# A decoder trunk on one core: the second expert product runs on a gathered list of picked experts instead of on all expert blocks

## The chip, the cores and the metric

One core of a Trainium2 chip runs the whole program. The metric is the device time of one execution in microseconds (us). TensorE (PE) multiplies, VectorE (DVE) and ScalarE (ACT) do elementwise work, GpSimd (POOL) some more of it, and SyncE (SP) issues DMA transfers in the order of its program. All arrays are float32.

## What is computed

Two layers, each with three token mixers (a recurrent one and two kinds of attention) and then an expert layer, on 256 tokens of 1024 features. Only the expert layer is touched. In the reference it is this, run on two tiles of 128 tokens, with 8 heads, 128 x 128 = 16,384 experts and 16 picks for each head:

```python
def block(zb):                                   # 128 tokens
    q = (zb @ wq).reshape(128, 8, 2, 128)
    s = jnp.einsum('thpd,hpnd->thpn', q, subkeys)
    s_top, i_top = lax.top_k(s, 16)
    cand = (s_top[:, :, 0, :, None] + s_top[:, :, 1, None, :]).reshape(128, 8, 256)
    score, flat = lax.top_k(cand, 16)
    ...
    expert = i1 * 128 + i2
    gate = jax.nn.softmax(score, axis=-1)
    h = jnp.einsum('thkd,td->thk', u_tab[expert], zb)
    act = gate * jax.nn.gelu(h, approximate=False)
    return jnp.einsum('thk,thkd->td', act, v_tab[expert])
```

So a token uses at most 128 of the 16,384 rows of `u_tab` and `v_tab`. The kernel doesn't gather rows for each token: it makes a dense matrix of activations, experts by tokens, that is zero where a token didn't pick an expert, and multiplies it by all of `v_tab`.

## The kernel before

Every float32 product is made of three products of rounded parts (`mm3`, L284 to L286): a value is split into a rounded `hi` (ScalarE, a cast) and the rest `lo` (VectorE, a subtraction), both at L280, and TensorE adds hi by hi, hi by lo and lo by hi. Weights come from memory in pieces of 128 x 1024 values, 512 KB: SP issues the load at L244 into a ring of `raw` tiles (3 slots), `load_split` splits it into `hi` and `lo` (2 sets, and a further set called `third` in part of the V phase), and a `raw` slot is free for the next load when its `lo` is made.

The expert layer (`peer`, L1044) has these stages, one after the other on TensorE:

- The query weights `wq` and the routing (`route`): scores, the top picks of each token, their gates. It leaves `sl` (which picks) and `gp` (the gates).
- The U phase, one `expert_h` (L1104) for each block of 128 experts, 128 blocks: a `ut` piece is loaded and split, 24 matmuls of 128 x 256 follow, and Gelu goes to the activations `HA` (blocks 0 to 47) or `HB` (48 to 127), experts on partitions, 256 tokens each.
- Beside the U phase, from block `SPLIT` = 48 on, `gate_map` (L1218): for each quad of tokens, VectorE makes one-hot rows (`oh`, L1233) and multiplies by the gates (L1236), TensorE makes 8 small f16 matmuls (L1241), which give the gate of each expert and token, and the activations are multiplied by it (L1244, L1248, L1250). There are 64 quads. `Pace` lets out 1.8 units of this work for each U block, and a quad costs 1.8, so one quad stands beside one block until they are used up. The later blocks are plain.
- The V phase, `accum` (L1000): for each of the 128 blocks, a `v` piece is loaded and split, the activations are split into `ah` and `al` (`a_of`, 2 buffers each), and 12 matmuls of 128 x 512 add to four accumulators, one for each token tile and half of the 1024 features (`sc`, `sc`, `tp`, `po`). Expert blocks are 128 rows of `v` in their order.

The order of instructions on each engine is set when the program is built, by a list scheduler that runs a timeline of its own, except where the code orders some explicitly. SP's DMAs take turns on 8 completion semaphores.

Of the kernel before, what the change touches and what calls it, by code (L numbers as in the profile page):

```python
# [21 lines left out]
L = 2  # L22
# [19 lines left out]
LAG = 1  # L42
ORDER = "rsrrrsrrcsrcrrrnrccrcsrcrrscrncsrrrgnrrrnaagSaSaSSagSgSaggSnggggSagSSnSaagaaaSgSgmSSSamamaSSaagSggSgggggSSmgmmgmmmmmmmmmmmmmmmmmm"
# [64 lines left out]

def layout(a):
# [36 lines left out]
    for h in range(H):  # L146
# [5 lines left out]
    c, hot, ext, iota = constants()  # L152
    d = dict(
# [4 lines left out]
        ut=a["peer_u"].reshape(L, NB, P, 8, P).transpose(0, 1, 4, 3, 2),  # L158
        v=a["peer_v"].reshape(L, NB, P, D),
# [9 lines left out]
        cst=c, eye=np.eye(P, dtype=np.float32), hot=hot, ext=ext, iota=iota,  # L169
# [26 lines left out]
class Kernel:  # L196
# [39 lines left out]
    def load(self, src):  # L236
        raw = self.ring.tile([P, D], F32, tag="raw", name="raw", bufs=RAW)
        n = 1
        for s in src.shape[1:]:
            n *= s  # L240
        v = raw[:, :n]
        if len(src.shape) == 3:
            v = v.rearrange("p (a b) -> p a b", a=src.shape[1])
        self.nc.sync.dma_start(v, src)  # L244
        return v

# [797 lines left out]
    def peer(self, l):  # L1044
        nc, I = self.nc, self.I
        act, dve, pe = nc.scalar, nc.vector, nc.tensor
        with ExitStack() as ctx:
# [26 lines left out]
            self.hdone, self.tok = 0, 0  # L1074
            run = Pace(self.gate_map(hp, (sl, gp), HA, HB), PACE_G)
            for b in range(SPLIT, NB):
                self.expert_h(l, b, blk(b), hp, self.tok)
                self.hdone += 1
                run(1)
            run(None)  # L1080

            def a_of(b):
                ah = hp.tile([P, T], F32R, tag="ah", name="ah", bufs=2)
                al = hp.tile([P, T], F32R, tag="al", name="al", bufs=2)
                self.split(blk(b), ah, al)
                return ah, al
# [4 lines left out]
            if l + 1 == self.layers:  # L1091
# [4 lines left out]
            self.xnew = self.accum(lambda b: I["v"][l, b], NB, a_of, lambda: self.load_x(self.xd[0]),  # L1096
                                     l + 1 < self.layers)
# [3 lines left out]
            if l + 1 == self.layers:  # L1101
                self.final(self.xnew, lnf)

# [9 lines left out]
    def route(self, rp, sub, qT, slots):  # L1113
# [21 lines left out]
        for t in range(2):  # L1135
# [29 lines left out]
            for n in range(2):  # L1165
# [12 lines left out]
                if n == 0:  # L1178
# [11 lines left out]
                    yield 0.8  # L1190
            gt = rp.tile([P, H, 16], F32, name="gt")
# [26 lines left out]
    def gate_map(self, hp, slots, HA, HB):  # L1218
# [7 lines left out]
        nc.gpsimd.tensor_copy(iota2, iota[:, :, None].to_broadcast([P, P, 2]))  # L1226
        for t0 in range(0, T, 4):
# [8 lines left out]
            dve.tensor_tensor(og, oh[:, 0:1].to_broadcast([P, 2, 2, P, 2]),  # L1236
                              g[:, :, :, None].to_broadcast([P, 2, 2, P, 2]), op=OP.mult)
            p = self.pt([P, 4, P], "sc")
            for j in range(4):
                for n in range(2):  # L1240
                    pe.matmul(p[:, j], lhsT=oh[:, 1, j // 2, :, j % 2], rhs=og[:, n, j // 2, :, j % 2], start=n == 0,  # L1241
                              stop=n == 1)
            pv = p.rearrange("p t i -> p i t")
# [8 lines left out]
            yield 1.8  # L1252

# [27 lines left out]
```

## Time and profile before

| what | before |
|---|---|
| median of 3 runs (lowest, highest) | 2372.96 us (2371.32, 2373.24) |
| the profiled execution: its time | 2373.9 us |
| its span, first to last instruction | 2372.1 us |
| TensorE busy | 2339.2 us, 99% of the span |
| VectorE, ScalarE, GpSimd busy | 72%, 50%, 3% |
| layer 0: `gate_map` matmuls, first to last quad | 540 to 792 us |
| layer 0: V matmuls | 836.80 to 1185.59 us |
| layer 1: V matmuls | 2013.41 to 2364.65 us |

Of the views, the table by stretch of time gives for each engine how long it was busy, the granted TensorE clock (1.00 is full speed), the share of time in which the 16 DMA engines were busy, and the rate at which data moved. The tables of instruction groups give a line, an engine, an operation, the tiles written and read, a count, the total and the mean time. TensorE's records overlap, because matmuls are pipelined, so the price of one matmul is read from the distance between starts.

### The profile page before, as it was taken

What the parts mean: (1) busy time and instruction counts of PE and PEld (TensorE: products, weight loads), DVE (VectorE), ACT (ScalarE), POOL (GpSimd) and SP (SyncE); (2) the same over time, 40 slices, a digit from 0 to 9 for tenths busy, and PEclk for the clock granted to TensorE, in tenths of its full rate; (3) what the DMA queues carried; (4) which work ended last, traced back from release to release, by engine and by line L of the source; (5) the groups of instructions that cost most, each with busy time, mean ns of one, the idle gap of its engine ahead of it and who ended that gap; (6) DMA issues with size and microseconds to landing.
All of it is one profiled execution on the core that took longest, in us unless ns stands there. A gap on an engine that the chain in (4) does not pass through costs nothing.

```text
span 2372.1 us, 43631 instructions
## 1 busy us (share of the span) xinstructions
PE 2339.2 (99%) x16838; PEld 2111.2 (89%) x16838; DVE 1698.7 (72%) x3691; ACT 1181.1 (50%) x2269; POOL 73.2 (3%) x107
## 2 busy tenths in 40 slices
PE   8999999999999999999999999999999999999998
PEld 8888889999999988888888888899999999888887
DVE  6678577995899666666666785779958996566665
ACT  5544344554444455555555443345545444555554
POOL 0001030000000000000000010300000000000000
PEclk9999899999999999999999998999999999999999
DMA  5643246555455566666645432455555555666664
GB/s 187 201 147 104 68 125 197 163 183 177 155 152 160 169 213 195 192 192 194 194 164 183 141 106 64 148 184 161 179 178 154 159 154 184 209 192 194 195 195 152
DMA packets 126008, 395.23 MB, mean 167 GB/s; under 512 B 25270, under 2 KB 30824, under 8 KB 125544
## 3 DMA queue, kind: packets, MB, share of 16 engines
q1 hardware_dynamic: 125512, 391.92, 53.1%
q8 instruction: 132, 2.16, 0.4%
q14 instruction: 76, 0.62, 0.1%
q10 hardware_dynamic: 288, 0.52, 0.1%
HBM read 387.39 MB, written 5.01 MB: 165 GB/s over the span
## 4 chain that ended last, share of the span: by engine, by line
PE 91%; DVE 4%; DMA 2%; ACT 1%; issue 1%; POOL 0%; SPq 0%; DVEq 0%; POOLq 0%; ACTq 0%
PE mm L284 16%; PE mm L286 15%; PE mm L285 15%; PE sc L285 6%; PE sc L286 5%; PE sc L284 5%; PE sc L1241 3%; PE tp L286 3%; PE tp L285 3%; PE po L285 3%; PE po L286 3%; PE tp L284 3%; PE po L284 3%; DVE lo L280 2%; PE sc L837 1%; DMA raw<-wa 1%
## 5 line engine op out<-in xcount | busy, mean ns | idle before, releaser
L280 ACT CAST hi<-raw 128x1024 fp32r<-128x1024 f32 (+1 forms) x609 | 637.4, 1048 | 679.5 <-PE mm L285 494.0
L280 DVE TENSOR_TENSOR lo<-raw,hi 128x1024 fp32r<-128x1024 f32 (+1 forms) x609 | 748.3, 1230 | 303.2 <-ACT hi L280 301.4
L284 PE MATMUL mm<-zh,hi 128*128 128x256 f32 x3056 | 885.9, 290 | 6.2 <-ACT HA L1107 3.7
L286 PE MATMUL mm<-zh,lo 128*128 128x256 f32 x3056 | 875.1, 286 | 3.3 <-DVE lo L280 3.3
L285 PE MATMUL mm<-zl,hi 128*128 128x256 f32 x3056 | 868.6, 284 | 0.0
L284 PEld LDWEIGHTS mm<-zh,hi 128*128 128x128 f32 x3056 | 587.6, 192 | 25.3 <-issue 11.8
L286 PEld LDWEIGHTS mm<-zh,lo 128*128 128x128 f32 x3056 | 586.7, 192 | 13.5 <-issue 5.7
L285 PEld LDWEIGHTS mm<-zl,hi 128*128 128x128 f32 x3056 | 587.7, 192 | 3.8 <-issue 2.9
L280 DVE TENSOR_TENSOR third<-raw,third 128x1024 fp32r<-128x1024 f32 x80 | 98.0, 1225 | 50.6 <-ACT third L280 50.6
L280 ACT CAST ah<-HB 128x256 fp32r<-128x256 f32 x160 | 65.2, 407 | 121.5 <-PE po L285 121.5
L280 DVE TENSOR_TENSOR al<-HB,ah 128x256 fp32r<-128x256 f32 x160 | 68.0, 425 | 76.5 <-PE po L286 76.5
L285 PE MATMUL sc<-lo,ah 128*128 128x512 f32 x362 | 115.8, 389 | 0.1
L284 PE MATMUL sc<-hi,ah 128*128 128x512 f32 x362 | 115.4, 389 | 0.0
L286 PE MATMUL sc<-hi,al 128*128 128x512 f32 x362 | 112.4, 389 | 0.0
L280 ACT CAST third<-raw 128x1024 fp32r<-128x1024 f32 x80 | 84.3, 1054 | 44.8 <-PE po L286 36.4
L1233 DVE TENSOR_TENSOR oh<-iota,sl 128x1024 f16<-128x1024 f16 x128 | 87.5, 685 | 6.2 <-PE sc L1241 4.2
L1236 DVE TENSOR_TENSOR oh<-oh,gp 128x1024 f16<-128x1024 f16 x128 | 87.3, 683 | 0.0
L1241 PE MATMUL sc<-oh 128*128 128x128 f16 x1024 | 81.5, 220 | 0.0
L285 PEld LDWEIGHTS sc<-lo,ah 128*128 128x128 f32 x362 | 67.9, 188 | 14.6 <-DVE lo L280 0.6
L286 PEld LDWEIGHTS sc<-hi,al 128*128 128x128 f32 x362 | 67.9, 188 | 14.0
L284 PEld LDWEIGHTS sc<-hi,ah 128*128 128x128 f32 x362 | 67.8, 188 | 14.0
L280 ACT CAST ah<-HA 128x256 fp32r<-128x256 f32 x96 | 38.8, 406 | 65.7 <-PE po L285 65.7
(420 smaller groups left out, 3617.3 us busy)
## 6 DMA issues: line engine op xcount, KB each, us to landing
raw<-ut SPq DMA_DIRECT2D x256, 512.0 KB, 3.6
raw<-v SPq DMA_DIRECT2D x256, 512.0 KB, 3.5
raw<-wa SPq DMA_DIRECT2D x102, 512.0 KB, 3.3
raw<-wq SPq DMA_DIRECT2D x32, 512.0 KB, 3.6
raw<-wbr SPq DMA_DIRECT2D x24, 512.0 KB, 3.5
raw<-cw SPq DMA_DIRECT2D x16, 512.0 KB, 4.1
raw<-wo SPq DMA_DIRECT2D x16, 512.0 KB, 4.7
btile<-bd SPq DMA_DIRECT2D x16, 256.0 KB, 4.3
```

Of the source, the lines that this page charges most:

```text
L280: return self.nc.scalar.copy(hi, src), self.nc.vector.tensor_tensor(lo, src, hi.bitcast(F32), op=OP.subtract)
L284: return [mm(p, lhsT=l[0], rhs=r[0], start=first, stop=False), mm(p, lhsT=l[0], rhs=r[1], start=False, stop=False), mm(p, lhsT=l[1], rhs=r ...
L285: mm(p, lhsT=l[0], rhs=r[1], start=False, stop=False),
L286: mm(p, lhsT=l[1], rhs=r[0], start=False, stop=last)]
L837: pe.matmul(p, lhsT=qs(j), rhs=keys[lo:lo + 64, 0:nbr, 0:n], start=True, stop=True)
L1233: dve.tensor_tensor(oh.rearrange("p n a i j -> p (n a) i j"), iota2[:, None].to_broadcast(full), two(sl), op=OP.is_equal)
L1236: dve.tensor_tensor(og, oh[:, 0:1].to_broadcast([P, 2, 2, P, 2]), g[:, :, :, None].to_broadcast([P, 2, 2, P, 2]), op=OP.mult)
L1241: pe.matmul(p[:, j], lhsT=oh[:, 1, j // 2, :, j % 2], rhs=og[:, n, j // 2, :, j % 2], start=n == 0, stop=n == 1)
```

## The change

The V phase multiplies, for each token tile, only rows that some token of that tile picked.

- The rows of `ut` and `v` are turned on the host: row r of block b goes to place (r + b) mod 128 of its block, so that one column of picks spreads over the partitions. `route` computes the same turned place (three more VectorE instructions).
- `gate_map` has 4 more matmuls for each quad (L1385). They add to `cnt`, which says for each expert and token tile whether somebody picked it.
- `lists` (L1399) follows the quads. On the 116 first blocks it classes each expert as picked by both tiles, by one only, or by none, ranks the experts of each class inside groups of four partitions, and sorts them: 15 `max` and 14 `match_replace` of 128 x 464 values, some 25 small VectorE instructions, and a few small matmuls. `rows` and `vrows` come out: for each partition a list of 116 row numbers, those of tile 0 only first, then both, then tile 1 only. `flag` is over zero when the classes don't fit the fixed lengths below.
- `keep` writes the finished activations of blocks 0 to 115 to `act` in memory, by SP, in pieces of 8 blocks by 128 tokens (512 KB, rows of 512 bytes). The first half of the tokens is written once 128 tokens are gated, the second after all 256.
- `experts_out` takes the place of `accum` here. 12 dense blocks (116 to 127) run first, with 12 matmuls each as before. Then 106 gathered items: item j takes column j of `rows`. GpSimd issues two indirect DMAs for each: 128 rows of `v` (4 KB each) and 128 rows of `act` (1 KB each), into slots laid out in `HA`'s room, 7 for `v` and 10 for `act`. Items 20 to 79 serve both token tiles (12 matmuls), items 0 to 19 tile 0 only and 80 to 105 tile 1 only (6 matmuls each), mixed evenly. Columns 106 to 115 are left out.
- Ahead of the 43rd item every engine reads `flag` and branches: the branch's body does what the fixed lengths leave out (396 matmuls, with single buffers), and is skipped when `flag` is zero.

The V phase has then 12 x 12 + 60 x 12 + 46 x 6 = 1140 matmuls of 128 x 512 in place of 1536.

```diff
+ND = 12
+NC = NB - ND
+FROM1, TO0, TO1 = 20, 80, 106
+IF_AT = 42
+CHUNK = 8
...
+    def gather(self, src, row, dst):
+        self.nc.gpsimd.indirect_dma_start(out=dst, out_offset=None, in_=src,
+                                          in_offset=bass.IndirectOffsetOnAxis(ap=row, axis=0))
...
+            def keep():
+                for h in range(2):
+                    if self.tok < P * (h + 1):
+                        continue
+                    ready = min(SPLIT + self.hdone, NC)
+                    while kept[h] < ready:
+                        b = kept[h]
+                        n = min(CHUNK, (SPLIT if b < SPLIT else NC) - b)
+                        if b + n > ready:
+                            break
+                        src = HA[:, b:b + n] if b < SPLIT else HB[:, b - SPLIT:b - SPLIT + n]
+                        nc.sync.dma_start(dA[b * P:(b + n) * P, h * P:(h + 1) * P].rearrange("(b p) t -> p b t", p=P),
+                                          src[:, :, h * P:(h + 1) * P])
+                        kept[h] += n
...
                 self.expert_h(l, b, blk(b), hp, self.tok)
                 self.hdone += 1
                 run(1)
+                keep()
             run(None)
...
-            self.xnew = self.accum(lambda b: I["v"][l, b], NB, a_of, lambda: self.load_x(self.xd[0]),
-                                     l + 1 < self.layers)
+            self.xnew = self.experts_out(l, hp, HA, blk, dA, l + 1 < self.layers)
...
+                raw, src = (cut(7 + n % 2, D), cut(46 + n % 2, T)) if rest else (cut(n % 7, D), cut(36 + n % 10, T))
+                self.gather(I["v"], self.vrows.bitcast(U32)[:, b:b + 1], raw)
+                self.gather(dA, self.rows.bitcast(U32)[:, b:b + 1], src)
+                if rest or n % 3 == 2:
+                    w = third[:, 0], third[:, 1]
+                else:
+                    w = [self.ring.tile([P, D], F32R, tag=tag, name=tag) for tag in ("hi", "lo")]
+                self.split(raw, *w)
...
+        for b in range(NC, NB):
+            both(ready(b, (0, 1), True))
+        self.deep = False
+        ahead = []
+        for n, (b, ts) in enumerate(seq):
+            if n == IF_AT:
+                ahead = [ready(*seq[n + k]) for k in range(2)]
+                flag = nc.values_load(self.flag, min_val=0, max_val=1 << 20)
+                with self.tc.If(flag > 0):
+                    for j in range(FROM1):
+                        both(ready(j, (1,), rest=True))
+                    for j in range(TO0, TO1):
+                        both(ready(j, (0,), rest=True))
+                    for j in range(TO1, NC):
+                        both(ready(j, (0, 1), rest=True))
+            both(ahead.pop(0) if ahead else ready(b, ts))
...
-            dve.tensor_tensor(og, oh[:, 0:1].to_broadcast([P, 2, 2, P, 2]),
-                              g[:, :, :, None].to_broadcast([P, 2, 2, P, 2]), op=OP.mult)
+            for n in range(2):
+                dve.tensor_tensor(og[:, n], oh[:, 0], g[:, n, :, None].to_broadcast([P, 2, P, 2]), op=OP.mult)
...
+                at = t0 + j
+                pe.matmul(cnt[:, at // P], lhsT=oh[:, 1, j // 2, :, j % 2], rhs=oh[:, 0, j // 2, :, j % 2],
+                          start=at % P == 0, stop=at % P == P - 1)
...
+        yield from self.lists(hp, cnt)
```

SP's order before, layer 0, from the end of the routing to the end of the V loads (tiles are named target first; `ut`, `v`, `wa` are weights, and x90 is 90 issues in a row):

```order
L244 DMA raw<-ut 128x1024 x38
L1225 DMA iota<-iota 128x128
L244 DMA raw<-ut 128x1024 x90
L244 DMA raw<-wa 128x1024
L244 DMA raw<-v 128x1024 x21
L232 DMA xt<-xd_116 128x1024 x2
L244 DMA raw<-v 128x1024 x107
```

and after, from the loads ahead of token 256 to the dense `v` loads (ahead of these rows, after the load that follows token 128, 6 writes from `HA` and 4 from `HB` stand in one row, and three more between the loads):

```order
L267 DMA raw<-ut 128x1024 x7
L1116 DMA act_6692<-HA 128x8x128 x5
L1116 DMA act_6692<-HB 128x8x128
L1116 DMA act_6692<-HA 128x8x128
L1116 DMA act_6692<-HB 128x8x128 x8
L267 DMA raw<-ut 128x1024 x3
L1116 DMA act_6692<-HB 128x4x128 x2
L1209 TENSOR_LOAD flagi
L1209 ISA x2
L267 DMA raw<-ut 128x1024 x8
L267 DMA raw<-wa 128x1024
L267 DMA raw<-v 128x1024 x12
```

The 90 loads in a row are cut up: 10 writes stand in a row ahead of the load that follows token 128, 15 in a row ahead of the load that follows token 256, and a read of the flag stands ahead of the last 8 `ut` loads.

VectorE at the second of those places, before (the last quads of layer 0, with a block's `lo` and its activation product `HB<-HB,gel` beside each):

```order
L1236 TENSOR_TENSOR oh<-oh,gp 128x1024
L1244 SCALAR_TENSOR_TENSOR HA<-HA,sc 128x48x4
L1248 SCALAR_TENSOR_TENSOR HB<-HB,sc 128x63x4
L280 TENSOR_TENSOR lo<-raw,hi 128x1024
L1111 TENSOR_TENSOR HB<-HB,gel 128x252
L1244 SCALAR_TENSOR_TENSOR HA<-HA,sc 128x48x4
L1248 SCALAR_TENSOR_TENSOR HB<-HB,sc 128x64x4
L280 TENSOR_TENSOR lo<-raw,hi 128x1024
```

and after (`ms`, `cf`, `off`, `over` belong to `lists`), from the last `lo` that stands ahead of the 15 writes' load:

```order
L307 TENSOR_TENSOR lo<-raw,hi 128x1024
L1247 TENSOR_TENSOR HB<-HB,gel 128x256 x2
L1432 TENSOR_TENSOR ms<-ms,off 128x464
L1449 TENSOR_SCALAR over<-off 128x1
L1450 TENSOR_SCALAR over<-off 128x1
L1451 TENSOR_SCALAR over<-off 128x1
L1433 TENSOR_TENSOR ms<-ms 128x464
L1435 TENSOR_REDUCE cf<-ms 128x116
L1438 TENSOR_SCALAR ms<-cf 128x116
L1439 TENSOR_SCALAR ms<-ms 128x116
L1440 TENSOR_SCALAR ms<-ms 128x116
L1247 TENSOR_TENSOR HB<-HB,gel 128x256
```

Here 32 instructions of the lists and of `HB` stand between two `lo`, and a part of the sort has come ahead of the next one.

GpSimd, which issued no DMA before, has this order behind the routing (layer 0; the pairs of the last two rows go on to the end of the phase):

```order
L1366 CAST iota_6725<-iota 128x256
L271 DMA HA<-act_6692,rows 128x256 x5
L271 DMA HA<-v,vrows 128x1024 x6
L271 DMA HA<-act_6692,rows 128x256
L271 DMA HA<-v,vrows 128x1024
L271 DMA HA<-act_6692,rows 128x256 x4
L271 DMA HA<-v,vrows 128x1024
L271 DMA HA<-act_6692,rows 128x256
L271 DMA HA<-v,vrows 128x1024
```

All of the V phase's loads but 12 have moved from SP's queue to GpSimd's.
## Rows read from the trace of the kernel before

**Rows 1.** Page, part 1: busy us (share of the span) and instructions of each engine.

```profile
PE 2339.2 (99%) x16838; PEld 2111.2 (89%) x16838; DVE 1698.7 (72%) x3691; ACT 1181.1 (50%) x2269; POOL 73.2 (3%) x107
```

**Rows 2.** Stretches of layer 0: U with quads, plain U, V (columns in the first line).

```profile
core 0: us, PE busy (x) PEld busy (x) DVE busy (x) ACT busy (x) POOL busy (x), PEclk, DMA share, GB/s
540.00:780.00 240.00, 240.00 (x2222) 237.42 (x2221) 197.88 (x371) 114.77 (x266) 0.00 (x0) 1.00 0.54 161
800.00:836.00 36.00, 34.86 (x291) 34.66 (x290) 18.14 (x25) 15.99 (x24) 0.00 (x0) 1.00 0.55 181
1000.00:1170.00 170.00, 170.00 (x751) 140.77 (x750) 103.02 (x126) 91.47 (x126) 0.00 (x0) 1.00 0.63 193
```

**Rows 3.** Waits of SP's queue: for whom, us in total, times, longest us.

```profile
SPq L244 <- DVE lo L280: 975.5, 361, 16.9
```

**Rows 4.** Timeline of PE, layer 0: start us, us, instruction; a quad, then V's ends.

```profile
779.93 0.28 PE L286 MATMUL mm<-zh,lo 128*128 128x256 f32 x1
...
781.01 0.28 PE L286 MATMUL mm<-zh,lo 128*128 128x256 f32 x1
781.14 0.63 PE L1241 MATMUL sc<-oh 128*128 128x128 f16 x8
781.58 0.36 PE L284 MATMUL mm<-zh,hi 128*128 128x256 f32 x1
...
836.80 0.63 PE L284 MATMUL sc<-hi,ah 128*128 128x512 f32 x2
...
1185.20 0.39 PE L286 MATMUL po<-hi,al 128*128 128x512 f32 x1
```

**Rows 5.** Waits of PE: for whom, us in total, times, longest us.

```profile
PE mm L325 <- DVE diag L323: 9.2, 4, 7.2
```

**Rows 6.** DMA issues: count, KB each, median us to landing.

```profile
raw<-ut SPq DMA_DIRECT2D x256, 512.0 KB, 3.6
raw<-v SPq DMA_DIRECT2D x256, 512.0 KB, 3.5
...
xd<-xt SPq DMA_DIRECT2D x6, 512.0 KB, 2.6
```

**Rows 7.** Page, part 5: instructions xcount | busy us, mean ns of one | idle before.

```profile
L280 ACT CAST hi<-raw 128x1024 fp32r<-128x1024 f32 (+1 forms) x609 | 637.4, 1048 | 679.5 <-PE mm L285 494.0
L280 DVE TENSOR_TENSOR lo<-raw,hi 128x1024 fp32r<-128x1024 f32 (+1 forms) x609 | 748.3, 1230 | 303.2 <-ACT hi L280 301.4
...
L280 DVE TENSOR_TENSOR al<-HB,ah 128x256 fp32r<-128x256 f32 x160 | 68.0, 425 | 76.5 <-PE po L286 76.5
```

**Rows 8.** A further instruction group of DVE, the same columns.

```profile
L1214 DVE MATCH_REPLACE8 S<-top,S 128x128 f32<-128x128 f32 x64 | 17.0, 277 | 0.0
```

**Rows 9.** Another stretch, the same columns as rows 2: loads in the mixer of layer 1.

```profile
1256.00:1259.40 3.40, 3.40 (x24) 2.63 (x23) 1.36 (x4) 1.85 (x4) 0.00 (x0) 1.00 0.86 325
```

**Rows 10.** Instruction groups of POOL, the same columns as rows 7.

```profile
L979 POOL TENSOR_TENSOR mg<-mg,gate 128x256 f32<-128x256 f32 x32 | 32.9, 1034 | 58.9 <-DVE st L699 32.0 <-DVE gate L977 26.9
...
L314 POOL TENSOR_TENSOR ss<-ss,neghalf 128x1 f32<-128x1 f32 x10 | 5.5, 554 | 1348.1 <-DVE ss L313 1346.4 <-DVE small L379 1.7
```

**Rows 11.** Tile blk: duration ns min/median/max of one line on DVE and on POOL.

```profile
L542 DVE TENSOR_TENSOR TQ<-blk,cst x4: 1225/2096/2973, 196.7 to 1378.4; 128x1024 f32<-128x1024 f32 x4
L542 POOL TENSOR_TENSOR TQ<-blk,cst x4: 2915/2919/2922, 196.8 to 1380.3; 128x1024 f32<-128x1024 f32 x4
```

**Rows 12.** Timeline of PE at the start of the span.

```profile
7.16 1.23 PE L325 MATMUL mm<-diag,xt 128*128 128x128 f32 x4 [7.16 <-DVE diag L323]
8.18 1.06 PE L325 MATMUL sm<-diag,xt 128*128 128x128 f32 x4
9.03 1.06 PE L325 MATMUL mm<-diag,xt 128*128 128x128 f32 x4
...
11.92 0.61 PE L325 MATMUL mm<-diag,xt 128*128 128x128 f32 x4
12.37 0.61 PE L325 MATMUL sm<-diag,xt 128*128 128x128 f32 x4
```

More of the change, by code (lines that the diff above doesn't have):

```diff
@@ L106, in constants, with quads @@
     return c, hot, ext, np.tile(i.astype(f), (P, 1))
+def quads():
+    i = np.arange(P)
+    same = i[:, None] % 32 == i[None, :] % 32
+    m = i // 32
+    q = np.zeros((P, 7, P), np.float32)
+    q[:, 0] = same & (m[:, None] < m[None, :])
+    q[:, 1] = same & (m[:, None] > m[None, :])
+    for n in range(4):
+        q[:, 2 + n] = same & (m[:, None] == n)
+    q[:, 6, :NC] = NC * 512 + m[:, None] * P + np.arange(NC)
+    q[:, 6, NC] = -65536.0 * m
+    q[:, 6, NC + 1] = 1.0
+    return q
 def layout(a):
@@ L152, in layout @@
     c, hot, ext, iota = constants()
+    turn = (r(P)[None, :] - r(NB)[:, None]) % P
+    skew = lambda w: w.reshape(L, NB, P, D)[:, r(NB)[:, None], turn]
     d = dict(
@@ L157, in layout @@
         wq=cols(a["peer_wq"], r(2048)),
-        ut=a["peer_u"].reshape(L, NB, P, 8, P).transpose(0, 1, 4, 3, 2),
-        v=a["peer_v"].reshape(L, NB, P, D),
+        ut=skew(a["peer_u"]).reshape(L, NB, P, 8, P).transpose(0, 1, 4, 3, 2),
+        v=skew(a["peer_v"]).reshape(L * NB * P, D),
         subk=a["peer_subkeys"].reshape(L, 16, P, P).transpose(0, 3, 1, 2),
@@ L168, in layout @@
         rel=a["rel_bias"],
-        cst=c, eye=np.eye(P, dtype=np.float32), hot=hot, ext=ext, iota=iota,
+        cst=c, eye=np.eye(P, dtype=np.float32), hot=hot, ext=ext, iota=iota, quad=quads(),
+        low=np.tile((r(P) % 32).astype(np.int32)[:, None], (1, NC)),
     )
@@ L1073, in peer @@
             blk = lambda b: HA[:, b] if b < SPLIT else HB[:, b - SPLIT]
-            self.hdone, self.tok = 0, 0
+            dA = self.dram.tile([NC * P, T], F32, name=f"act{l}")
+            self.l, self.hdone, self.tok = l, 0, 0
+            kept = [0, 0]
+            def keep():
[12 more added lines that the diff above has]
+                        kept[h] += n
             run = Pace(self.gate_map(hp, (sl, gp), HA, HB), PACE_G)
@@ L1079, in peer @@
                 run(1)
+                keep()
             run(None)
[L1082 to L1086, printed above, removed]
+            keep()
+            assert kept == [NC, NC]
             if l + 1 < self.layers:
@@ L1190, in route @@
                     yield 0.8
+            dve.tensor_tensor(e, e, i1, op=OP.add)
+            wrap = rp.tile([P, H, 16], F32, name="wrap")
+            dve.tensor_scalar(wrap, e, float(P), float(P), op0=OP.is_ge, op1=OP.mult)
+            dve.tensor_tensor(e, e, wrap, op=OP.subtract)
             gt = rp.tile([P, H, 16], F32, name="gt")
@@ L1226, in gate_map @@
         nc.gpsimd.tensor_copy(iota2, iota[:, :, None].to_broadcast([P, P, 2]))
+        cnt = self.pt([P, 2, P], "tp")
         for t0 in range(0, T, 4):
```

142 lines of the change are left out of this document (added).

## The prediction, made before the changed kernel ran

> **What bounds the kernel now.** I read the page's busy times first: TensorE multiplies for 99% of the span, and no other engine is busy over 72% [rows 1]. So time goes only where matmuls go, unless something new makes TensorE wait. Then the three stretches of layer 0 [rows 2]: TensorE is busy 240 of 240 us beside the quads and 170 of 170 us in V, at the full granted clock; VectorE has 18% free beside the quads, half in the plain U blocks, 39% in V; the DMA engines are busy 0.54 to 0.63 of the time. SP mostly waits for a ring slot [rows 3], so loads come when room is there, and memory isn't what limits. What I must ask is which of these reserves the change eats up.
>
> The sum is made against the profiled execution, 2373.9 us (span 2372.1); the median of the runs is 0.9 us lower. All terms are for one layer, and there are two.
>
> **Matmuls taken away.** V runs from 836.80 to 1185.59 us, 348.8 us for 1536 matmuls, 0.227 us each [rows 4]. 396 fewer: **-89.9 us**. This holds if TensorE still goes at its own pace: 1140 matmuls then take 259 us, the mean gathered item 996 x 0.227 / 106 = 2.13 us.
>
> **Matmuls added.** A quad's 8 small matmuls begin at 781.14 and the next block's at 781.58: 0.055 us each [rows 4]. 256 more: **+14.1 us**, on TensorE in a stretch where it has no gap [rows 2]. The split gate product costs VectorE no more elements, and the routing's three extra instructions lie where I see no wait of TensorE's over 7.2 us in all of the span [rows 5]: 0.
>
> **The writes of the activations.** A queue is served in SP's order: 10 writes stand ahead of a `ut` load at token 128, 15 at token 256. Their price isn't in the trace. At the V loads' share, 0.63 busy at 193 GB/s [rows 2], full engines would move 306 GB/s (193/0.63), and 512 KB takes 1.71 us. TensorE's cover is the three `raw` slots: a block is 24 x 0.12 = 2.88 us, with its quad now 3.5 us [rows 4]. Token 128: 10 x 1.71 - 3 x 3.5 = 7 us. Token 256: 15 x 1.71 - 3 x 2.88 = 17 us. Together **+24 us**. Bounds: with two more blocks of cover in `hi` and `lo`, 0 and 11 us; with writes in 512-byte rows at half the pace, 24 and 43 us. I stay at 24, because the one large write seen lands no later than a load, 2.6 against 3.6 us [rows 6]. The other five writes stand alone among loads: 0.
>
> **The lists.** They are VectorE work behind the last quad, and TensorE doesn't need them before the gathers. An instruction of 256 values takes 0.425 us, one of 1024 1.230 us, and a match_replace of 128 0.277 us [rows 7, 8], so one of 464 about 0.64 us (an estimate from these). 36 of these and some 18 small ones at 0.27: 28 us. The 16 plain blocks last 46 us and leave VectorE half free, 23 us [rows 2]; the second stall adds 17. So the lists hide behind a stall that is paid already: **0**. Without that stall they would cost 28 - 23 = 5 us themselves. SP's read of the flag waits for them too, but the loads behind it need slots that VectorE frees later still.
>
> **The gathers.** 12 dense blocks (12 x 2.72 = 33 us) run while the first 17 gathers are issued. Then an item needs 640 KB and two gathers. VectorE needs 1.23 + 0.43 = 1.66 us of 2.13 [rows 7]. DMA at 306 GB/s needs 2.14 us, just TensorE's pace; where the engines were busiest they moved 325 GB/s at 0.86 [rows 9], that is 378 GB/s and 1.73 us. If the 1 KB rows of `act` cost double for each byte, the item takes 2.57 us at the lower rate: 0.44 x 106 = +47 us; at the higher rate nothing is lost. I take **+10 us**, near the cheap end, because the busiest row is the one most like a queue that is never empty. GpSimd's own price for a gather isn't in the trace either. Its instruction on one value for each partition takes 0.554 us, on 256 values 1.034 us, on 1024 values 2.919 us [rows 10, 11]. A gather reads one value for each partition, so the nearest rows are the first two: at 1.034 us GpSimd would finish V in 30 + 195 x 1.034 + 8 = 240 us (30 until the slots come free in turn, 195 gathers still to issue, 8 for the end), less than 259: it hides.
>
> By the Trainium skill's "DMA: Bandwidth & Descriptors", section "Latency and other measured facts", such a DMA has a first byte after about 1 us, put down there to the descriptors being made in software; by that price V is 30 + 195 + 8 = 233 us and the sum the same. No run so far shows it.
>
> **The branch.** All engines empty their queues around it and GpSimd waits until its gathers have landed. TensorE has two items in hand, 4.3 us. Bounds: the 1.1 us that it lost where U turns into V (36.00 - 34.86) [rows 2], and a load plus a split, 3.5 + 1.0 + 1.2 = 6 us [rows 6, 7]. I take **+4 us**.
>
> **Slow starts.** After its one long wait TensorE ran four matmuls in 1.02 and 0.85 us, and from about 11 us on in 0.45 us [rows 12]: 3.7 us at half its pace, 1.8 us lost. Three stalls a layer: **+5 us** (0 to 7).
>
> **Sum.** -89.9 + 14.1 + 24 + 0 + 10 + 4 + 5 = -32.8 us a layer, -66 us in both: 2308 us.
>
> **Rival 1: GpSimd makes descriptors slower than that.** V is then 38 + 195p for a price p of one gather. It decides from 259 us on, p = 1.13; the whole gain is gone when V takes 259 + 10 + 32.8 = 302 us, p = 1.35. At p = 1.6: 350 us, 91 - 10 = 81 us more, +48 a layer, **2470 us**, slower. For it: 1.35 lies between two rows, and 212 gathers of 128 rows each are much for an engine that is busy 3% now. Against it: a gather doesn't read 256 values. Chance 0.15.
>
> **Rival 2: VectorE and GpSimd shut each other out.** The same subtraction took VectorE 1.225 us or up to 2.973 us when GpSimd ran its half beside it, 2.919 us [rows 11]: one waited for the other. In V both work all the time: VectorE's `lo` and `al` and GpSimd's two gathers. One after the other an item takes 1.66 + 2 x 0.554 = 2.76 us, V 33 + 106 x 2.76 = 326 us, 67 - 10 = 57 us more: +24 a layer, **2422 us**, slower. It decides when the part of a gather that holds VectorE off is over 0.44 us ((302 - 33) / 106 = 2.54; (2.54 - 1.66) / 2). [...] Chance 0.11.
>
> The Trainium skill's "SBUF — State Buffer", section "Who interferes with whom", says that a VectorE instruction with two inputs in SBUF, such as these subtractions, contends with a GpSimd one that reads SBUF, and that the second to start blocks fully. That speaks against this change; rows 11 agree with it for elementwise work, and none shows it for a gather. By this rule the whole gather counts, and the time is the 2422 us above.
>
> **Rival 3: the writes are absorbed.** SP's writes overlap loads, the two stalls cost 0 and 5 us (the lists), one slow start is left: -89.9 + 14.1 + 5 + 10 + 4 + 2 = -55 a layer, **2264 us**. For it: the DMA engines are busy 0.55 of the time in U [rows 2], and the order leaves loads in flight. Chance 0.23.
>
> **Rival 4: it doesn't do what it says, because the branch is taken.** 396 matmuls come back, as 56 items with one buffer each: load, split and multiply in turn, at least 1.0 + 1.2 + 1.4 us each, 3.6 x 56 = 202 us more: some 2710 us. Worked out from the reference on its inputs, the classes fit in both layers with some per cent to spare (at least 92 rows for tile 0 only of every four partitions, 80 needed; at most 411 picked at all, 424 allowed). Chance 0.02.
>
> **How the numbers follow.** The forecast, gathers at TensorE's pace and both bursts paid in part, has 0.44, between 2285 and 2340. Rival 3 and mixtures towards it 0.23, between 2240 and 2285. The same mechanism with dear writes or 1 KB rows, 24 + 47 in place of 24 + 10 or 67 in place of 24, ends at 2382 or 2394: 0.05. Rivals 1, 2 and 4: 0.28. The range 2245 to 2440 leaves out the tail of rival 3 (0.04), most of rival 1 (0.12) and rival 4 (0.02). A measurement of this kernel can tell about 0.2% (5 us) from no change. Faster by more: 0.44 + 0.23 = 0.67. Slower by more: rivals 1, 2, 4 and the dear bounds, less 0.03 that falls within 5 us of no change: 0.30. Same: 0.03.
>
> **What would show it.** In the table by stretch, V of layer 0 should last 265 to 280 us with TensorE busy over 94% and DMA near 0.9; in the waits of TensorE, two gaps of some 7 and 17 us for `lo` at the writes; GpSimd's gathers about 1 us each, with gaps between them. Wrong it would be if TensorE waits through V for `hi` and `lo` while GpSimd has no gap (rival 1), if `lo` has become much longer than 1.23 us (rival 2), if no gap stands at the writes (rival 3), or if matmuls of `rest` show (rival 4).

## The result, and the profile after

The change makes the kernel slower: 2429.06 us median (2427.15 to 2434.28) against 2372.97, a ratio of 1.0241, 95% interval 1.0224 to 1.0259. The profiled execution took 2434.28 us, its span is 2432.5, against 2372.1 before: +60.4 us. The prediction was 2308, faster; the measured time lies near the upper end of its range of 2245 to 2440.

The page of the changed kernel, part 1, two lines of part 3 (queues: packets, MB, share of the 16 engines) and groups of part 5, columns as in [rows 1, 7]:

```profile
PE 2275.7 (94%) x16602; PEld 1998.9 (82%) x16602; DVE 1715.5 (71%) x3933; ACT 1145.4 (47%) x2233; POOL 539.0 (22%) x533
...
q1 hardware_dynamic: 153032, 301.72, 39.4%
q0 software_dynamic: 40704, 138.96, 18.4%
...
L271 POOL DMA_INDIRECT HA<-act,rows x212 | 250.6, 1182 | 773.4 <-ACT ready L307 336.5
L307 DVE TENSOR_TENSOR lo<-HA,hi 128x1024 fp32r<-128x1024 f32 x142 | 174.0, 1226 | 138.7 <-ACT hi L307 138.5
L271 POOL DMA_INDIRECT HA<-v,vrows x212 | 214.8, 1013 | 87.8 <-issue 42.4
```

TensorE fell from 99% to 94% of a longer span, and GpSimd rose from 3% to 22%. Where the time went, by stretch of the changed kernel (quads; first and second burst of writes; V in three pieces), columns as in [rows 2]:

```profile
540.00:780.00 240.00, 235.33 (x2256) 232.27 (x2254) 185.97 (x395) 110.71 (x242) 0.00 (x0) 0.99 0.57 175
700.00:715.00 15.00, 10.33 (x101) 9.80 (x100) 9.04 (x21) 4.16 (x10) 0.00 (x0) 0.87 0.86 273
800.00:850.00 50.00, 32.59 (x281) 31.90 (x280) 37.28 (x82) 14.65 (x30) 0.00 (x0) 0.81 0.85 255
920.00:1000.00 80.00, 78.00 (x327) 59.74 (x325) 52.47 (x68) 46.50 (x68) 61.62 (x58) 1.00 0.76 234
1000.00:1050.00 50.00, 38.35 (x146) 26.82 (x144) 23.41 (x30) 20.91 (x32) 32.20 (x32) 0.96 0.70 223
1050.00:1200.00 150.00, 132.38 (x493) 89.38 (x494) 83.53 (x107) 72.09 (x108) 115.64 (x105) 0.97 0.77 235
```

In V TensorE's records nearly fill the stretch, but its matmuls are few: 493 in 150 us is 0.30 us each, where [rows 4] give 0.227. The timeline of TensorE has V of layer 0 between these two matmuls (at 877.35 and 1209.22), and the end of the long wait at the second burst:

```profile
844.88 0.58 PE L311 MATMUL mm<-zh,hi 128*128 128x256 f32 x1 [16.25 <-ACT hi L307]
846.85 0.58 PE L311 MATMUL mm<-zh,hi 128*128 128x256 f32 x1 [1.17 <-ACT hi L307]
...
877.35 0.63 PE L311 MATMUL sc<-hi,ah 128*128 128x512 f32 x2
...
1209.22 0.39 PE L313 MATMUL po<-hi,al 128*128 128x512 f32 x1
```

So V starts 40.55 us later than before (836.80) and lasts 331.9 us in place of 348.4: only 16.5 us of the 89.9 came. Layer 0 ends +24.0. In layer 1 V lasts 337.4 us in place of 350.9 and all else takes 44.9 us more, +31.4; the end of the program behind the last V matmul is 5.0 us longer, for which no cause was looked for. 24.0 + 31.4 + 5.0 = 60.4.

Who ended the waits of ScalarE and of GpSimd in V of layer 0 (880 to 1205 and 920 to 1205; us, times, longest):

```profile
ACT hi L307 <- DMA HA<-v,vrows: 72.4, 51, 2.0
ACT third L307 <- DMA HA<-v,vrows: 48.0, 26, 6.7
ACT ah L307 <- PE po L312: 27.5, 22, 4.6
...
POOL HA L271 <- issue: 43.3, 142, 0.3
POOL HA L271 <- DMA HA<-v,vrows: 12.0, 12, 8.7
POOL HA L271 <- DMA HA<-act,rows: 6.1, 20, 0.3
POOL HA L271 <- DVE al L307: 3.4, 11, 0.3
```

ScalarE waits for gathered rows, 120 us. GpSimd waits for nobody once the slots come free in turn: its gaps are 0.30 us, one behind each gather, three of 0.6 to 0.8 us at the start, and 8.65 us once at the branch. If the rows landed too late, or memory were too slow, slots would stay full and GpSimd would wait for them. Its timeline where the slots first come free, and at the branch:

```profile
897.87 0.95 POOL L271 DMA_INDIRECT HA<-v,vrows  x1 [0.30 <-issue]
918.67 0.95 POOL L271 DMA_INDIRECT HA<-act,rows  x1 [19.85 <-DVE al L307]
...
928.52 0.95 POOL L271 DMA_INDIRECT HA<-v,vrows  x1 [0.30 <-issue]
929.78 0.95 POOL L271 DMA_INDIRECT HA<-act,rows  x1 [0.30 <-issue]
...
1032.14 1.17 POOL L271 DMA_INDIRECT HA<-act,rows  x1 [0.30 <-issue]
1033.62 1.16 POOL L271 DMA_INDIRECT HA<-v,vrows  x1 [0.31 <-issue]
1035.08 0.95 POOL L271 DMA_INDIRECT HA<-act,rows  x1 [0.30 <-issue]
1044.68 0.94 POOL L271 DMA_INDIRECT HA<-v,vrows  x1 [8.65 <-DMA HA<-v,vrows]
```

18 gathers lie before 918.67, and the last of the 212 starts at 1196.38: (277.71 - 8.65) / 193 = 1.394 us from one gather to the next. That makes V: 41.3 to the 19th gather, 193 x 1.394 = 269.1, 8.65 at the branch, 12.8 from the last gather to the last matmul, 331.9 us.

### The profile page after: what moved, and what is told of

Read it like the earlier page. It is cut to its first block, busy times and chain, and to the rows that moved or that the text cites. A ratio compares the mean times of both kernels' runs of the same rounds, so it can differ in the third digit from the quotient of the medians.

```text
span 2432.5 us, 43965 instructions
## 1 busy us (share of the span) xinstructions
PE 2275.7 (94%) x16602; PEld 1998.9 (82%) x16602; DVE 1715.5 (71%) x3933; ACT 1145.4 (47%) x2233; POOL 539.0 (22%) x533
## 5 line engine op out<-in xcount | busy, mean ns | idle before, releaser
L307 ACT CAST hi<-raw 128x1024 fp32r<-128x1024 f32 (+1 forms) x451 | 470.4, 1045 | 469.1 <-PE mm L312 303.5
L307 DVE TENSOR_TENSOR lo<-raw,hi 128x1024 fp32r<-128x1024 f32 (+1 forms) x451 | 555.0, 1232 | 179.7 <-ACT hi L307 178.3
L271 POOL DMA_INDIRECT HA<-act,rows x212 | 250.6, 1182 | 773.4 <-ACT ready L307 336.5
L307 DVE TENSOR_TENSOR lo<-HA,hi 128x1024 fp32r<-128x1024 f32 x142 | 174.0, 1226 | 138.7 <-ACT hi L307 138.5
L271 POOL DMA_INDIRECT HA<-v,vrows x212 | 214.8, 1013 | 87.8 <-issue 42.4
L307 ACT CAST hi<-HA 128x1024 fp32r<-128x1024 f32 x142 | 148.9, 1049 | 156.7 <-DMA HA<-v,vrows 146.5
L307 DVE TENSOR_TENSOR third<-HA,third 128x1024 fp32r<-128x1024 f32 x70 | 85.8, 1226 | 96.3 <-ACT third L307 96.3
L307 ACT CAST third<-HA 128x1024 fp32r<-128x1024 f32 x70 | 73.4, 1048 | 115.5 <-DMA HA<-v,vrows 93.8
L307 DVE TENSOR_TENSOR al<-HA,ah 128x256 fp32r<-128x256 f32 x212 | 89.1, 420 | 24.7 <-DVEq L1210 8.6
L1378 DVE TENSOR_TENSOR oh<-oh,gp 128x512 f16<-128x512 f16 x256 | 96.5, 417 | 0.3
```

The source lines that it names most:

```text
L271: self.nc.gpsimd.indirect_dma_start(out=dst, out_offset=None, in_=src, in_offset=bass.IndirectOffsetOnAxis(ap=row, axis=0))
L307: return self.nc.scalar.copy(hi, src), self.nc.vector.tensor_tensor(lo, src, hi.bitcast(F32), op=OP.subtract)
L1378: dve.tensor_tensor(og[:, n], oh[:, 0], g[:, n, :, None].to_broadcast([P, 2, P, 2]), op=OP.mult)
```

## The experiments

**Theory 1**: GpSimd's pace sets V. **Rivals**: memory can't give 640 KB for an item in 2.13 us; VectorE and GpSimd take turns; the branch or the writes are what is dear. Each run has an edit of the changed kernel. V is that of layer 0. The last column counts, from 880 to 1150 us, the completion signals (semaphore increments) of TensorE, ScalarE and VectorE that the trace has over 0.1 us after the instruction's end; it became the main point of the second half. In the runs with late signals the trace has fewer signals than instructions (ScalarE's in c2_after_third: 1803 for 1967), and an instruction without one of its own is counted by the next one, so the column tells the two sorts of runs apart and is no exact tally. Runs of one set ran together.

| set | run | median us | ratio to before, 95% | V, us | late signals |
|---|---|---|---|---|---|
| first | changed kernel | 2429.06 | 1.0241 [1.0224, 1.0259] | 331.9 | 0 of 584 |
| 1 | e1_act_dense | 2317.06 | 0.9779 [0.9752, 0.9807] | 278.4 | 81 of 707 |
| 1 | e2_no_lo | 2473.45 | 1.0439 [1.0385, 1.0493] | 350.2 | 96 of 305 |
| 1 | e3_no_branch | 2458.56 | 1.0363 [1.0323, 1.0403] | 347.6 | 244 of 546 |
| 1 | e4_spread | 2448.25 | 1.0339 [1.0311, 1.0367] | 345.3 | 206 of 549 |
| 2 | c1_after_again | 2424.77 | 1.0218 [1.0197, 1.0238] | 329.0 | 0 of 587 |
| 2 | e5_both_dense | 2326.64 | 0.9793 [0.9771, 0.9815] | 274.7 | 0 of 702 |
| 2 | e6_mix32 | 2333.40 | 0.9835 [0.9812, 0.9857] | 297.6 | 0 of 663 |
| 2 | e7_mix32_spread | 2321.19 | 0.9785 [0.9764, 0.9806] | 293.8 | 0 of 676 |
| 3 | c2_after_third | 2468.14 | 1.0389 [1.0343, 1.0436] | 352.8 | 213 of 540 |
| 3 | e3b_no_branch | 2463.21 | 1.0362 [1.0334, 1.0391] | 342.8 | 193 of 565 |
| 3 | e4b_spread | 2446.60 | 1.0315 [1.0297, 1.0332] | 349.0 | 235 of 545 |
| 3 | e2b_no_lo | 2475.97 | 1.0425 [1.0404, 1.0446] | 357.2 | 102 of 300 |
| 4 | c4_after | 2454.75 | 1.0366 [1.0334, 1.0399] | 346.2 | 222 of 552 |
| 4 | c4_no_lo | 2468.33 | 1.0413 [1.0373, 1.0453] | 356.4 | 92 of 297 |
| 4 | c4_no_branch | 2454.88 | 1.0369 [1.0323, 1.0416] | 341.4 | 245 of 557 |
| 4 | c4_mix32_spread | 2344.95 | 0.9885 [0.9854, 0.9916] | 311.7 | 215 of 641 |
| 5 | c5_no_lo | 2475.46 | 1.0413 [1.0374, 1.0453] | 357.1 | 88 of 301 |
| 5 | c5_v_dense | 2330.72 | 0.9828 [0.9798, 0.9857] | 274.4 | 2 of 706 |

**Half of the gathers, or none.** e1_act_dense has the first of these two edits, c5_v_dense the second, e5_both_dense both (`rest` is the branch's body, which doesn't run):

```diff
-                self.gather(dA, self.rows.bitcast(U32)[:, b:b + 1], src)
+                if rest:
+                    self.gather(dA, self.rows.bitcast(U32)[:, b:b + 1], src)
+                else:
+                    nc.sync.dma_start(src, dA[b * P:(b + 1) * P])
...
-                self.gather(I["v"], self.vrows.bitcast(U32)[:, b:b + 1], raw)
+                if rest:
+                    self.gather(I["v"], self.vrows.bitcast(U32)[:, b:b + 1], raw)
+                else:
+                    nc.sync.dma_start(raw, I["v"][(l * NB + b) * P:(l * NB + b + 1) * P])
```

> GpSimd gathers only the rows of v; the rows of act come as plain SP loads of 128 rows in a row of memory (512 of 640 KB and all packets of an item stay, but the wrong rows of act are multiplied). Theory 1, GpSimd's pace sets the V phase (a gather every 1.40 us, 212 of them): 106 are left, GpSimd needs about 150 us, TensorE's 259 us decide, V of layer 0 falls from 332 to 260 to 280 us and the time by 105 to 140 us, to 2290 to 2325. Rival, the landing of the rows (bytes, packets, slots) sets it: the bytes are the same, V stays within 10 us of 332 and the time within 20 us of 2429.

> No gathers at all outside the branch: the rows of v and act for the 106 items are loaded by SP as plain blocks (so wrong rows are multiplied); the same 1140 matmuls, lists, writes, branch. Theory 1 (GpSimd's 1.40 us for a gather is what V lost, and nothing else in the change is that dear): V falls to 262 to 280 us, the total to 2290 to 2315 us, no late signals. Rival (memory: 640 KB an item can't be had in 2.13 us whoever issues it): V stays over 300 us, 2350 us or more.

> The counterpart of e1_act_dense: SP loads the rows of v as plain blocks (so wrong rows of v are multiplied), GpSimd gathers those of act alone, 106 gathers a layer in place of 212. Theory 1 (GpSimd's pace): V 265 to 285 us, 2300 to 2330 us. If signals are late in this set and go with the number and pace of the gathers: few late ones, as in e1_act_dense, and the same time. If they go with the 1 KB rows: many late ones, V 300 us or more, 2360 us or more.

V is 278.4, 274.7 and 274.4 us, 54 to 57 less than in the changed kernel's first trace and 51 to 55 less than in c1_after_again (sets 1 and 5 have no run of the changed kernel), with the same 1140 matmuls, the same bytes and the same VectorE work; but the rows that SP loads stand in a row in memory. A stretch of V (920 to 1000 us) of e1_act_dense, of e5_both_dense and of c5_v_dense:

```profile
920.00:1000.00 80.00, 80.00 (x345) 64.45 (x344) 58.61 (x74) 52.51 (x75) 33.94 (x37) 1.00 0.89 299
```

```profile
920.00:1000.00 80.00, 80.00 (x345) 64.45 (x344) 56.69 (x72) 50.99 (x73) 0.00 (x0) 1.00 0.89 287
```

```profile
920.00:1000.00 80.00, 80.00 (x344) 64.48 (x343) 57.71 (x73) 51.07 (x74) 46.13 (x37) 1.00 0.90 295
```

TensorE runs at its own pace, 345 matmuls in 80 us (0.232 each), and the DMA engines move 287 to 299 GB/s where the changed kernel had 234. So memory could give the rows, as far as one kind of them is scattered; no run has both kinds scattered at this pace. Without gathers ScalarE waits for TensorE again, as the waits in V of e5_both_dense (892 to 1160 us) show:

```profile
ACT ah L307 <- PE po L312: 63.2, 67, 2.9
ACT hi L307 <- PE po L313: 14.2, 27, 0.5
...
ACT hi L307 <- DMA HA<-v: 5.8, 11, 0.5
```

With one gather an item it makes no difference which: the 4 KB rows of v or the 1 KB rows of act. GpSimd waits for free slots again: in e1_act_dense 110 us for VectorE's `lo` and `third` from 930 to 1140 us, where the changed kernel has its gaps of 0.30 us. Theory 1 holds: V hangs on the number of gathers, not on bytes. (c5_v_dense took 2330.72 us, where 2300 to 2330 were expected. e5_both_dense took 2326.64 and not 2315 us at most, because its V starts 15.5 us later than in c1_after_again beside it; TensorE's waits for hi between 800 and 900 us are 24.5 us in place of 17.4, and the rest was not followed up.)

**VectorE's subtractions away.** In the gathered items hi stands in for lo:

```diff
-                self.split(raw, *w)
+                if rest:
+                    self.split(raw, *w)
+                else:
+                    nc.scalar.copy(w[0], raw)
+                    w = [w[0], w[0]]
...
-            self.split(src, *a)
+            if dense or rest:
+                self.split(src, *a)
+            else:
+                nc.scalar.copy(a[0], src)
+                a = [a[0], a[0]]
```

> In the gathered items VectorE's two subtractions are left out and the rounded part is multiplied in the place of the rest (wrong low parts, the same matmuls), so VectorE is idle while GpSimd gathers. Theory A, VectorE's subtractions and GpSimd hold each other up: all gathers take 0.95 us like the shortest now (mean now 1.18 for act, 1.01 for v), so a gather comes every 1.25 us and V is 25 to 30 us shorter in each layer, 2370 to 2385. Theory B, a gather takes its time alone: gathers keep their mean, V stays within 8 us and the time within 15 us of 2429.

> The changed kernel without VectorE's subtractions in the gathered items, as in e2_no_lo (hi stands in for lo, so the result is not the kernel's). Theory A: the gathers take 0.95 us each and stand 1.25 us apart in place of 1.40, V is 195 x 0.15 = 29 us shorter in each layer as long as GpSimd still sets the pace: 2365 to 2385 us. Theory B: late signals again and about 2470 us.

> The changed kernel without VectorE's subtractions in the gathered items (hi stands in for lo, so the result is not the kernel's). With prompt signals, theory 1 (GpSimd's pace sets V): gathers of 0.95 us, 1.25 us apart, V some 29 us shorter in each layer, 2365 to 2385 us. Rival with prompt signals (something else than GpSimd's pace, such as the time from a gather's issue to its use, sets V): within 10 us of the control. With late signals: 2470 us, as in e2_no_lo.

> The changed kernel without VectorE's subtractions in the gathered items (the result is not the kernel's). If its trace shows prompt signals: GpSimd's pace sets V, which becomes some 29 us shorter in each layer, 2365 to 2385 us; rival, something else sets V, 2415 to 2430 us. If signals are late: 2465 to 2476 us, as in the other three runs.

The gathers did become shorter, 0.966 and 0.954 us in place of 1.182 and 1.013, as these groups of e2_no_lo show:

```profile
L271 POOL DMA_INDIRECT HA<-act,rows x212 | 204.9, 966 | 854.9 <-ACT ready L307 337.3
L271 POOL DMA_INDIRECT HA<-v,vrows x212 | 202.2, 954 | 84.6 <-issue 50.3
```

V did not: 350 to 357 us in all four runs. (One execution of e2b_no_lo took 8874 us, for which no cause was looked for.) The control of set 3 shows why.

**The changed kernel again, and the branch and the bursts beside it.** The runs named no_branch have the If block deleted. Those named spread let `keep` write at most one piece for each U block:

```diff
                         kept[h] += n
+                        if self.hdone < NB - SPLIT:
+                            return
```

> The branch and its body are left out, all else is the same; on this input the body doesn't run. GpSimd's gap of 8.65 us at the branch should go. If GpSimd sets the pace of V, all of that comes back: 8 to 14 us in each layer, 2400 to 2414. If TensorE's waits at the branch (4.4 and 6.2 us) are all of its price: 8 to 12 us in both layers together, 2417 to 2421. If the 5 us that the span has grown behind the last instruction of VectorE belong to the branch's code, 5 us more fall away.

> The same writes, but SP issues at most one of 512 KB for each block of U, where 10 and 15 stand in a row now. If the rows of writes in front of the loads are the cause of TensorE's two waits (4.1 and 16.3 us in layer 0) and of the low clock behind them, the waits go and U ends 18 to 26 us earlier in each layer: 2377 to 2393. If the lists on VectorE hold the blocks up, the second wait stays above 8 us and the time within 20 us of 2429.

> The changed kernel itself, unchanged, beside the kernel before on the chip of this set. In the traces of e2_no_lo, e3_no_branch and e4_spread the semaphore signals of TensorE, ScalarE and VectorE come up to some microseconds after the instruction's end while gathers are issued, in the first trace of the changed kernel never over 0.02 us. Theory A: this belongs to the chip (or to how the program was loaded on it), not to those edits: the same kernel shows late signals here too and takes 2440 to 2470 us. Theory B: it comes from the edits, because the gathers are issued further ahead of their use there: 2425 to 2435 us, V of layer 0 332 us, no late signals.

> The changed kernel once more, as the control beside the three repeats of this set. In the set of e1 to e4 engines' signals came up to microseconds late while gathers were issued; in the set of c1, e5, e6 and e7 none did, not even with gathers issued well ahead of their use (e6, e7). Theory A (lateness belongs to the chip or the loading of that set): 2420 to 2432 us where the repeats beside it are prompt, 2440 us or more with late signals where they are late. Theory B (it comes from those edits): 2420 to 2432 us without late signals, with late ones in the repeats.

> The changed kernel without the branch, as in e3_no_branch. Theory A: no late signals now, V loses the 8.65 us gap of the gathers and some slow start, 7 to 11 us a layer less than the changed kernel beside it: 2402 to 2415 us. Theory B: late signals again and about 2458 us.

> The changed kernel with the writes of the activations spread, at most one piece for each U block, as in e4_spread. Theory A: V starts some 8 to 14 us earlier in each layer and, if the lists are ready as much earlier, ends as much earlier: 2398 to 2415 us. Theory B: late signals again and about 2448 us. Rival for theory A's gain: GpSimd starts its gathers when the lists are done and sets the end of V, so an earlier start of V alone gives nothing: 2420 to 2430 us.

> The changed kernel as the control of this set: 2423 to 2432 us and no signal over 0.1 us late if this is a set with prompt signals, 2445 to 2476 us with signals microseconds late beside the gathers if it is one of the other sort.

> The changed kernel without the branch. With prompt signals: 7 to 11 us a layer less than the control, 2402 to 2415 us. With late signals: within 15 us of the control.

Theory A in its first form (late signals come with the chip, so the unchanged kernel shows them too) failed in c1_after_again, which came out as theory B had it: 2424.77 us and no late signal. In its second form (they belong to a set of runs, not to an edit) it held: the unchanged kernel takes 2468.14 and 2454.75 us with late signals in sets 3 and 4, while the medians of the kernel before stay between 2370 and 2376. The chip alone doesn't decide, for sets 2 and 3 ran on the same one. (Each of the four sets with late signals has a no_lo run in it, and the two without have none; no run tests whether that matters.) What differs is seen in V of c2_after_third; its timeline, without the lines of PEld:

```profile
1127.92 1.05 ACT L307 CAST hi<-HA 128x1024 fp32r<-128x1024 f32 x1 [1.72 <-PE po L312]
...
1128.99 1.23 DVE L307 TENSOR_TENSOR lo<-HA,hi 128x1024 fp32r<-128x1024 f32 x1 [0.59 <-ACT hi L307]
1129.05 0.63 PE L313 MATMUL po<-third,al 128*128 128x512 f32 x1
1129.60 1.43 POOL L271 DMA_INDIRECT HA<-act,rows  x1 [0.31 <-issue]
...
1136.34 0.94 POOL L271 DMA_INDIRECT HA<-v,vrows  x1 [0.30 <-issue]
1137.10 0.40 ACT L307 CAST ah<-HA 128x256 fp32r<-128x256 f32 x1 [8.14 <-remote]
...
1137.56 1.22 PE L311 MATMUL sc<-hi,ah 128*128 128x512 f32 x2 [7.88 <-ACT ah L307]
```

TensorE, ScalarE and VectorE all stand still from 1130.2 to 1137.1 us, and only GpSimd goes on. ScalarE's `ah` needs TensorE's last matmul, which ended at 1129.68; its signal is in the trace at 1137.08, 7.4 us later, and ScalarE starts 0.02 us behind that. The table of waits for ScalarE in V of c2_after_third (880 to 1225 us) has turned around against the changed kernel's first trace (`remote` is a signal that the profile puts down to no instruction), and GpSimd waits for free slots (930 to 1215 us):

```profile
ACT ah L307 <- PE po L312: 44.4, 42, 2.5
ACT ah L307 <- remote: 36.1, 12, 8.1
...
ACT hi L307 <- DMA HA<-v,vrows: 7.2, 7, 1.7
...
POOL HA L271 <- DVE al L307: 18.1, 19, 3.4
```

In stretches of 20 us of c2_after_third signals are late where gathers are issued (19 of 27 in 880 to 900, 14 gathers), and next to never where none are (1 of 38 in 900 to 920, 0 of 61 in 1220 to 1240). TensorE's clock suffers too. During the halt it is at its lower level, 1.2 GHz:

```profile
1129.00:1141.00 12.00, 4.12 (x10) 2.77 (x9) 1.65 (x3) 1.49 (x3) 6.78 (x8) 0.50 0.75 234
```

It had fallen at 1127.96, before the halt, in the second of two waits of TensorE, 1.1 and 1.0 us. Over 880 to 1225 us the granted clock is 0.92 in the mean, where c1_after_again has 0.98 from 880 to 1200 us.

So what e2, e3 and e4 give against the first measurement of the changed kernel says nothing; only the controls of their sets count. Against those: no subtractions +8 and +14 us, no branch -5 and 0 us, spread writes -21.5 us (2446.60 against 2468.14; V starts 6.7 us earlier in layer 0). The executions of c2_after_third lie between 2452 and 2476 us and those of c4_after between 2454 and 2461, so the first four of these differences lie within that spread or at its edge; the last is clear of it, but its size is rough. That in these sets the signals made V long, so that a shorter gather or a missing branch had nothing to give, fits GpSimd's waits above, but no run isolates it. With prompt signals no_lo and no_branch were never seen.

**Fewer gathers, all rows right.** 32 dense blocks in place of 12, 8 ahead and 24 mixed evenly among 87 gathered items; e7_mix32_spread and c4_mix32_spread have the spread writes as well:

```diff
-ND = 12
+ND = 32
-FROM1, TO0, TO1 = 20, 80, 106
-IF_AT = 42
+FROM1, TO0, TO1 = 16, 67, 87
+IF_AT = 36
...
-        for b in range(NC, NB):
-            both(ready(b, (0, 1), True))
+        dense = list(range(NC, NB))
+        for _ in range(8):
+            both(ready(dense.pop(0), (0, 1), True))
+        later = len(dense)
...
+            while dense and (later - len(dense) + 1) * (len(seq) - 8) <= (n + 1) * later:
+                both(ready(dense.pop(0), (0, 1), True))
```

> 32 dense blocks in place of 12, 8 of them first and 24 mixed evenly among 87 gathered items: 174 gathers and 1212 matmuls a layer, all rows right. Theory 1: GpSimd's 174 gathers of 1.40 us (244 us) now lie under TensorE's 275 us; V lasts 277 to 292 us and the total is 2325 to 2350 us, if signals are prompt. If late signals are what makes V long beside gathers (theory A on this chip), TensorE still waits and the total is 2350 to 2400 us. Rival (TensorE's waits are VectorE's and GpSimd's in turn): 2.76 us for each of 87 items and 2.72 for 32 dense blocks, 327 us, 2420 us.

> As e6_mix32, and the writes of the activations at most one piece of 512 KB for each U block. The two stalls of TensorE at the writes (4.7 and 17.4 us) should fall to under 10 us together; V starts 8 to 12 us earlier than in e6_mix32 and the total is 10 to 25 us lower. Rival: V takes the time back, because its lists and gathers are not ready any earlier: the same total within 5 us.

> 32 dense blocks mixed among 87 gathered items, writes spread, as in e7_mix32_spread. With prompt signals 2315 to 2327 us as there. With late signals, if these cost by the number of gathers: V of the changed kernel is 16 to 20 us longer with them for 212 gathers, so some 15 us a layer for 174, 2345 to 2355 us; if the mixed dense blocks give TensorE other work while signals are late: under 2335 us.

V is 297.6 and 293.8 us with 1212 matmuls (275 us at TensorE's pace), and TensorE is at work again while GpSimd has time to spare: it waits for free slots. The stretch of V, a line of TensorE's waits over the span and one of GpSimd's from 920 to 1140 us, e7_mix32_spread:

```profile
920.00:1000.00 80.00, 79.85 (x341) 63.55 (x340) 53.49 (x67) 46.55 (x67) 53.32 (x51) 1.00 0.82 266
...
PE mm L311 <- ACT hi L307: 17.6, 7, 6.2
...
POOL HA L271 <- DVE lo L307: 18.4, 20, 2.2
```

e7_mix32_spread is 2.2% faster than the kernel before, and 12.2 us faster than e6_mix32: of the spread writes 10 to 25 were expected (V of layer 0 starts 5.6 us earlier, less than the 8 to 12 expected). With late signals it keeps 1.15%. It beats both kernels, and is the form in which this change pays.

## Why the prediction was wrong, point by point

The range holds the result by luck: the forecast's own mechanism ended at 2394 us at its dearest, and 2429 lies in the range only because this was drawn wide enough for rival 2 and a part of rival 1.

- **Matmuls taken away, -89.9 a layer**: right as a bound. Where nothing else holds V, it is 274.7 us (e5_both_dense): 259 and 15.7 for DMA, branch and slow starts, which had 10 + 4 + a part of 5.
- **Matmuls added and writes, +14.1 and +24**: right. The waits at the two bursts were 0.57 + 4.10 and 16.25 + 1.17 us where 7 and 17 stood, and V starts 40.55 us later, where the sum has 14.1 + 24 and two slow starts of 1.8, 41.7. The spread writes confirm about half of the bursts' price: from 700 to 870 us TensorE's waits fall from 22.2 us in c2_after_third to 11.9 in e4b_spread, and V starts 6.7 us earlier. In what is left, five writes still stand in a row (from 828.90 us).
- **Lists, 0**: right. The first gather starts at 873.46, before V's first matmul.
- **Gathers, the DMA half, +10**: if anything too dear. The engines moved 287 to 303 GB/s at 0.89 to 0.92 busy with one kind of rows scattered or none, and TensorE's only waits of 0.15 us or more in V of e5_both_dense and c5_v_dense are those at the branch, 4.2 and 4.0 us. Both kinds scattered were not seen at that pace.
- **Gathers, GpSimd's half, "it hides"**: this step failed. The price of one gather was taken as 1.034 us, the busy time of the nearest row, and its busy time is in fact close to that (1.182 and 1.013, mean 1.10; 0.94 at least). But V goes by the distance of two gathers, and that has 0.30 us more in which GpSimd does nothing the profile shows: 1.394 us. The trace of the kernel before has GpSimd instructions in a row, but elementwise ones, and there the next starts as the last ends (the row below this list: three in 3.39 us without a gap). So the 0.30 us belong to the gathers, not to any two instructions in a row, and no row of before could show them, since GpSimd issued no DMA there. What fills them is open. By the prediction's own 38 + 195p, V at p = 1.394 is 310 us, 51 over the 259; the price is past 1.35, where it had the whole gain end. The other 22 us: the gathers go on after 41.3 us and not 30 (+11.3), 193 are left and not 195 (-2.8), the end takes 12.8 and not 8 (+4.8), and the branch lies on GpSimd's path (+8.65).
- **The branch, +4**: the wait of TensorE is 4.2 us in e5_both_dense, as predicted. In the changed kernel it was mis-sized, since GpSimd had become the bound and lost 8.65 us. Its price was put on TensorE's path only.
- **Rival 1** had the mechanism, the place and the turning point, at a price below its 1.6. **Rival 2** had a true half with the wrong payer: VectorE's `lo` stays at 1.226 us, and GpSimd pays, 0.14 us a gather (1.10 with the subtractions, 0.96 without), some 27 us in V by 193 x 0.14. This is an estimate: the runs without subtractions all have late signals, and against c2_after_third (1.07) it is 0.11. The rival also priced a gather at 0.554 us where the forecast had 1.034; at 1.034 its item would take 3.73 us, and the gathers of one item are 2.79 apart.

The three instructions in a row of the kernel before, on GpSimd:

```profile
323.64 3.39 POOL L979 TENSOR_TENSOR mg<-mg,gate 128x256 f32<-128x256 f32 x3
```

A gather holds GpSimd for 0.94 us where VectorE leaves it alone. The Trainium skill's "DMA: Bandwidth & Descriptors", section "Latency and other measured facts", gives about 1 us to the first byte. The prediction took this for the pace, which is 1.394 us; and the trace doesn't agree with it as a delay either: in the changed kernel the first packet of gathered rows starts 3.45 us after the first gather of layer 0, and 1.68 us after the gather at 918.67, when no other gathered rows were on their way. Its "SBUF — State Buffer", section "Who interferes with whom", says that the second of the two to start blocks fully when the GpSimd instruction reads SBUF, and also that a probe saw no stall of a DMA by `tensor_tensor`, which the prediction left out. e2_no_lo lies between: it agrees that they contend and shows a mean cost of 0.14 us, not a whole subtraction of 1.23.

## What to carry to other kernels

Price an instruction that is issued in a row by the distance of two starts, not by its busy time, and where no trace has two of its kind in a row, put the missing gap into the range and not into the tail. When an idle engine is given a stream of work, ask for its whole pace against the engine it feeds (here 2 x 1.394 us against 2.13 us an item), and mix in work that doesn't need it until it has time to spare. Run the unchanged kernel in each set of runs: between sets 2 and 3 the same program was 43 us apart.

## What was not expected of the hardware

- A gather of 128 rows costs GpSimd the same for 4 KB and 1 KB rows where VectorE leaves it alone: 0.954 and 0.966 us in e2_no_lo, and 0.30 us behind it.
- Beside streams of gathers the completion signals of the other engines can come late, up to 7.4 us in the example, in some sets of runs and not in others. With half the gathers there were few (81 of 707) or next to none (2 of 706, in a set in which c5_no_lo had 88 of 301). Of the edited kernels only e5_both_dense has no gathers; it has no late signals either, but in a set in which no run had any. In sets 3 and 4 the changed kernel was 30 to 43 us slower with them than in c1_after_again. What decides between the two sorts of set is open; so is why the mixed kernel had none in set 2 and 215 of 641 in set 4 while its loss was only 24 us.
